# A hybrid decoder block on one Trainium2 core: the first token half normed ahead of the second, two of v's seven products beside it, and another issue order at three later stages

## The chip, the cores and the metric

The kernel runs on one core of one Trainium2 chip. The metric is the device time of one execution in microseconds (us). Engines are named as in the profile: PE (TensorE, the matrix engine), DVE (VectorE), ACT (ScalarE), POOL (GpSimd) and SP (SyncE, which here only issues DMAs, in the order of its queue, and waits on a semaphore before a DMA where it must). SBUF is the memory on the chip, PSUM the accumulators behind PE.

## The reference

One layer of a decoder block over 1024 tokens of width 1024, in float32, with three sub-layers. Every sub-layer norms its input (RMSNorm), and norms its output again before it is added to the stream.

1. Token mixing. One projection h @ w_in is split into q, k, v of a stick-breaking attention (16 heads), into z, x|B|C and dt of a state-space mixer (32 heads, 4 groups, chunks of 128 tokens), and into two gates. Each branch is projected to 1024 columns, gated, summed, and projected once more.
2. Cross-attention with 4 heads of 256 to 256 memory tokens.
3. A SwiGLU feed-forward with 2816 hidden columns.

The part of the reference that bears on this change is this:

```python
h = rms_norm(x, g_pre_mix[l])
q, k, v, z, xbc, dt_raw, ga, gs = _split(h @ w_in[l], IN_SIZES)
...
o_ssm = ssd_branch(z, xbc, dt_raw, ...)
merged = sigmoid(ga) * (o_att @ w_br_att[l]) + sigmoid(gs) * (o_ssm @ w_br_ssm[l])
x = x + rms_norm(merged @ w_mix_out[l], g_post_mix[l])
h = rms_norm(x, g_pre_xa[l])
x = x + rms_norm(memory_cross_attention(h, mem_n, w_xq[l], w_xkv[l], w_xo[l]), g_post_xa[l])
```

## The kernel before

**Products in three passes.** A float32 operand is split into a high part, rounded to PE's fast float32 form (`hi_sb`, on ACT or POOL), and the rest (`lo_of`, on DVE or POOL). A product is then three matmuls: high by high, high by low, low by high.

**Seven products for eight.** The projections of the first sub-layer go by the Winograd form of Strassen's scheme: the normed tokens are cut into four blocks of 512 features by 512 tokens, b11, b21 (the first token half) and b12, b22 (the second), and the weights into four blocks as well. Seven products of sums of them replace eight. The sums on the token side are t1 to t4. They need both halves: t1 = b12 - b11, t2 = b22 - t1, t3 = b22 - b12, t4 = b21 - t2. Their high and low parts stay in SBUF; those of b12 go to scratch in DRAM (`hb_d`).

**The first stage** (L262 to L351). Chunks of 128 tokens are normed: ACT squares and sums (L301), POOL makes the reciprocal root in two small operations (L166, L167), DVE scales (L302), PE turns eight blocks of 128 x 128 (L308). `chunk_pair` does this for chunk c of the first half and chunk c + 4 of the second at once, makes all parts of both (L319 and L320 in `put`, L325, L331 to L336), and multiplies both with the dt columns (`pdt`, L99 to L101, 48 small matmuls for the pair, stored to `dt_d` at L349). Four pairs run; no product of v runs beside them.

**v and z** (L353 to L457). `token_major` makes one third of v|z at a time, 512 + 512 columns. Its weights come in four blocks of two loads of 512 KB each (`zr`, L268). The order of the products is b11, t2, b21, t1, t3, b22, t4. Each product is four steps in k; a step splits one 128 x 512 piece of weights and feeds 12 matmuls, so a product is 48 matmuls. t2's weights are s2 = a21 + a22 - a11, and s1 = a21 + a22 and s3 = a11 - a21 are made first (L416 to L420, DVE for the first third). For the first third all eight loads are issued ahead of the norms, from a pool of ten tiles.

**The feature-major part** (from L461) makes x|B|C, gates, q and k in pairs of 128 columns. `winograd_weights` (L188) loads two tiles `wr` (L194) and makes four sums of weights on POOL (L197 to L200), then splits seven weights. For the first pair POOL splits the first three of them. Its tiles lie where the pools of v and z lay.

**The state-space stage** (from L846). `prep(n)` for one chunk and group loads rows of a small matrix (`colrows`, `keyrows`), whose product (`dec`, L922) holds the exponents of the decay. Both tiles hold constant rows beside the loaded ones: eight rows of a unit matrix come by DMA (`own`, L865) and the loaded sums stand in rows 0 and 1 (L914). `memory` (L1040, L1045) loads and norms the 256 memory tokens; it stands ahead of the loop that calls `prep`.

**The merge** (from L1186) multiplies the attention's output with w_br_att; weights come through `load_split` (L106, tiles `wraw`, `whi`). **Cross-attention** (from L1302) makes all queries, then loads v's projection of the memory (`vx_d`), then the scores (`soft`, L1338 to L1344), their turns (L1352) and the mix.

**What sets the order.** Each engine runs its own instructions in a fixed order that a scheduler worked out when the kernel was built, from the order in which the code issues them, their dependences and the tiles of the pools. A tile that is used again waits for its last reader; a pool that is opened where another one was closed waits for the readers of that space.

Of the kernel before, what the change touches and what calls it, by code (L numbers as in the profile page):

```python
# [30 lines left out]
FILL_LEFT, FILL_RIGHT = 128, 224  # L31
# [3 lines left out]
def hybrid_block(ctx, tc, a, out, dbg=None):  # L35
# [84 lines left out]
    pst0 = ExitStack()  # L120
    prp = pool(pst0, "prm")
    prm1 = mk(prp, [P, P], F32, "prm1")
    prm2 = mk(prp, [P, P], F32, "prm2")
    V.memset(prm1, 0.0)
    V.memset(prm2, 0.0)
    nc.sync.dma_start(prm1[0:96, :], a["conv_w"][0].rearrange("t (f p) -> (t f) p", p=P))
    rows = {}
    r0 = 0
    for nm, n in (("conv_b", 24), ("g_ssm_norm", 16)):
        nc.sync.dma_start(prm2[r0:r0 + n, :], a[nm][0].rearrange("(f p) -> f p", p=P))  # L130
        rows[nm] = r0
        r0 += n
    prmT = mk(cp, [P, 256], F32, "prmT")
    with tc.tile_pool(name="ps_prm", bufs=2, space=PSUM) as pp:
        for i, t in enumerate((prm1, prm2)):
            ps = mk(pp, [P, P], F32, "pprm")
            T.transpose(ps, t, ident)
            V.tensor_copy(prmT[:, i * P:(i + 1) * P], ps)
    pst0.close()
# [9 lines left out]
    nc.sync.dma_start(dsk, a["d_skip"][0].partition_broadcast(P))  # L149

# [3 lines left out]
    G.memset(mone, -1.0)  # L154
    stats = pool(ctx, "stats", 16)
# [96 lines left out]
    with ExitStack() as pa:  # L252
# [8 lines left out]
        rp = pool(pz, "zraw", 10, side="right")  # L261

        def block(r0, c0):
# [8 lines left out]
        def blocks(c0):  # L272
            return block(0, c0), block(0, c0 + HALF), block(512, c0 + HALF), block(512, c0)

        with ExitStack() as p1:
            t4 = pool(p1, "t4x0", 4)
            tt = pool(p1, "tcomb", 6)
            bt = pool(p1, "b12t", 4)
            mp = pool(p1, "memp")
            mt4 = pool(p1, "t4mem", 2)  # L280
            psp = pool(p1, "ps1", 2, PSUM)
            gx = load_gain(mp, "g_pre_mix")
# [6 lines left out]
            for c in (0, 4, 1, 5):  # L289
                load_x(c)  # L290
            wd = mk(mp, [P, KT, 32], F32, "wd")
            nc.sync.dma_start(wd, colblock(w_in, C_DT, 32))
            wdh, wdl = [mk(mp, [P, KT, 32], F32R, n) for n in ("wdh", "wdl")]
# [3 lines left out]
            def normed(c, eng):  # L297
# [13 lines left out]
            def chunk_pair(c):  # L311
# [31 lines left out]
                for i, q in enumerate(((q11, q21), (q12, q22))):  # L343
                    for k in range(KT):
                        hi, lo = q[k // 4]
                        mm3(pdt[0:32, i * P:(i + 1) * P], wdh[:, k, :], wdl[:, k, :], hi[:, k % 4, :], lo[:, k % 4, :], k == 0, k == KT - 1)
# [1344 lines left out]
```

## Time and profile before

| | |
|---|---|
| runs | 2629.86, 2631.71, 2632.2 us (median 2631.71) |
| the profiled execution | 2629.05 us, span 2627.3 us, mean granted PE clock 0.985 |
| PE busy | 2512.0 us, 96% of the span |
| DVE, ACT, POOL busy | 1821.2, 1152.6, 883.5 us |
| data moved by DMA | 271.86 MB, mean 103 GB/s |
| first transposes of tokens on PE | at 13.34 us |
| first product of v on PE | at 56.57 us |
| first matmul of the feature-major part | at 287.67 us |
| `dec` after its longest wait | at 1126.93 us |

How to read it: times are from the start of the span. A row of the waits names the engine and the instruction that waited, who released it, and the us in total, times and longest. A row of a timeline gives start and duration, and in brackets the idle time ahead of it with its releaser. Rows of groups give busy time, mean ns of one, and the idle time ahead. Rows of windows give for a stretch its length and then, engine by engine, busy time and (x) instructions, then the granted PE clock as a share of full speed, the share of the DMA engines and the GB/s.

### The profile page before, as it was taken

To read this page: it belongs to the slowest core of one execution; us is meant where nothing else is said; L and a number is where in the kernel's file an instruction comes from. 1 tells how busy PE (TensorE), PEld (TensorE's weight loads), DVE (VectorE), ACT (ScalarE), POOL (GpSimd) and SP (SyncE) were. 2 spreads that over 40 slices of the span, in tenths; PEclk is the share of its full clock that TensorE was granted. 3 is DMA by queue.
4 is the path that set the end of the run, shared out by engine and by line. 5 is a ranking of instruction groups with operands and counts; after the bars stand their busy time and mean duration, and the time that the engine had idled before them with its cause. 6 is when DMAs were issued, how large, how long until landed. Compare 5 with 4: busy or idle time off the path is not lost. (4 is left out here: it accounts for less than half of the span.)

```text
span 2627.3 us, 32746 instructions
## 1 busy us (share of the span) xinstructions
PE 2512.0 (96%) x12090; PEld 2082.1 (79%) x12090; DVE 1821.2 (69%) x2125; ACT 1152.6 (44%) x2044; POOL 883.5 (34%) x678
## 2 busy tenths in 40 slices
PE   5999999999999999989999999998999999999997
PEld 4888887787788888777888878887787888887786
DVE  7456778766598898677888654415459666666997
ACT  5333455555466665455544312314333333333342
POOL 5212544443111211154555230101114333324763
PEclk8999999999999999989999999999999999999999
DMA  5331442433422322255322461321232232324223
GB/s 174 113 108 53 129 139 91 120 104 105 121 71 70 84 69 69 85 172 183 110 90 70 129 198 66 118 75 41 88 117 72 77 96 73 96 73 152 96 107 134
DMA packets 240491, 271.86 MB, mean 103 GB/s; under 512 B 14751, under 2 KB 171048, under 8 KB 239946
## 3 DMA queue, kind: packets, MB, share of 16 engines
q1 hardware_dynamic: 240330, 269.76, 32.2%
q8 instruction: 95, 1.56, 0.2%
q14 instruction: 66, 0.54, 0.1%
HBM read 192.37 MB, written 68.82 MB: 99 GB/s over the span
## 5 line engine op out<-in xcount | busy, mean ns | idle before, releaser
L733 DVE TENSOR_TENSOR_SCAN n<-n,mask 128x128 f32<-128x128 f32 (+7 forms) x128 | 176.7, 1405 | 10.1 <-ACT n L732 7.1
L96 DVE TENSOR_TENSOR sw<-sf,sw 128x512 fp32r<-128x512 f32 x150 | 132.4, 895 | 64.5 <-ACT sw L93 64.2
L197 POOL TENSOR_TENSOR sf<-wr,wr 128x512 f32<-128x512 f32 x38 | 59.6, 1570 | 271.3 <-DMA wr<-in_w_gu_dram 125.8
L93 ACT ACTIVATE sw<-sf 128x512 fp32r<-128x512 f32 x150 | 92.1, 626 | 115.4 <-PE mm L223 96.9
L752 ACT ACTIVATE wth<-tr,mone 128x512 fp32r<-128x512 f32 x192 | 111.0, 581 | 72.2 <-PE tr L749 70.6
L753 DVE SCALAR_TENSOR_TENSOR wtl<-tr,wth 128x512 fp32r<-128x512 f32 x192 | 101.6, 546 | 38.8 <-ACT wth L752 37.4
L93 ACT ACTIVATE sw<-wr 128x512 fp32r<-128x512 f32 x113 | 71.0, 629 | 128.9 <-PE mm L223 126.8
L223 PE MATMUL mm<-h,sw 128*128 128x512 f32 x320 | 124.3, 389 | 1.2 <-DVE sw L96 1.2
L221 PE MATMUL mm<-h,sw 128*128 128x512 f32 x320 | 122.2, 390 | 2.9 <-ACT h L93 1.5
L222 PE MATMUL mm<-h,sw 128*128 128x512 f32 x320 | 124.6, 389 | 0.3 <-DVE h L96 0.3
L99 PE MATMUL mm<-oth,bw 128*128 128x512 f32 (+1 forms) x320 | 121.2, 379 | 0.1
L101 PE MATMUL mm<-oth,bw 128*128 128x512 f32 (+1 forms) x320 | 118.7, 372 | 1.4 <-DVE bw L96 1.3
L96 DVE TENSOR_TENSOR sw<-wr,sw 128x512 fp32r<-128x512 f32 x113 | 101.6, 900 | 25.9 <-ACT sw L93 17.9
L100 PE MATMUL mm<-otl,bw 128*128 128x512 f32 (+1 forms) x320 | 118.1, 369 | 0.0
L96 DVE TENSOR_TENSOR zl<-zr,zh 128x512 fp32r<-128x512 f32 x84 | 67.6, 810 | 72.0 <-ACT zh L93 71.9
L501 DVE SCALAR_TENSOR_TENSOR b<-b,prmT,b 128x1023 f32<-128x1023 f32 (+2 forms) x72 | 107.2, 1489 | 13.4 <-ACT b L499 12.7
L166 POOL TENSOR_SCALAR rstd<-ms 128x1 f32<-128x1 f32 x82 | 34.6, 422 | 236.0 <-ACT x L1239 110.0
L89 POOL TENSOR_SCALAR v<-va 128x512 fp32r<-128x512 f32 x16 | 20.1, 1260 | 275.1 <-PE av L762 148.0
L732 ACT ACTIVATE n<-sc 128x512 f32<-128x512 f32 (+1 forms) x192 | 89.3, 486 | 48.3 <-PE sc L731 24.4
L93 ACT ACTIVATE zh<-zr 128x512 fp32r<-128x512 f32 x84 | 52.4, 630 | 113.5 <-PE mb L407 55.3
L99 PE MATMUL p<-bw,h 128*128 128x512 f32 x256 | 98.9, 391 | 3.3 <-DVE x L1241 2.4
L101 PE MATMUL p<-bw,h 128*128 128x512 f32 x256 | 100.1, 392 | 0.0
(593 smaller groups left out, 8274.9 us busy)
## 6 DMA issues: line engine op xcount, KB each, us to landing
wr<-in_w_gu_dram SPq DMA_DIRECT2D x80, 256.0 KB
wr<-in_w_in_dram SPq DMA_DIRECT2D x36, 512.0 KB
zr<-in_w_in_dram SPq DMA_DIRECT2D x24, 512.0 KB
gu_d<-t SPq DMA_DIRECT2D x44, 256.0 KB
wraw<-in_w_in_dram SPq DMA_DIRECT2D x20, 512.0 KB
x<-in_x_dram SPq DMA_DIRECT2D x16, 512.0 KB
zs_d<-zo SPq DMA_DIRECT2D x32, 256.0 KB
xs_d<-b SPq DMA_DIRECT2D x32, 256.0 KB
```

What stands on the lines that cost most here:

```text
L93: A.activation(o, i, AF.Copy)
L96: eng.tensor_tensor(o, i, hi.bitcast(F32), ALU.subtract)
L99: first = T.matmul(ps, sh, mh, start=start, stop=False)
L100: T.matmul(ps, sh, ml, start=False, stop=False)
L101: T.matmul(ps, sl, mh, start=False, stop=stop)
L221: T.matmul(ps, w[0][:, k, :], b[0][:, k, :], start=first and k == 0, stop=False, skip_group_check=True)
L222: T.matmul(ps, w[0][:, k, :], b[1][:, k, :], start=False, stop=False, skip_group_check=True)
L223: T.matmul(ps, w[1][:, k, :], b[0][:, k, :], start=False, stop=last and k == 3, skip_group_check=True)
L501: V.scalar_tensor_tensor(acc[:, sh:], y[:, :S - sh], cw(3 - sh, f), acc[:, sh:], ALU.mult, ALU.add)
L733: V.tensor_tensor_scan(nt[:, 0:L][:, ::-1], nt[:, 0:L][:, ::-1], mask[:, S - L:][:, ::-1], 1.0, ALU.mult, ALU.max)
L752: A.activation(wh[:, t0 * P:], pt[:, t0 * P:], AF.Identity, bias=mone)
L753: V.scalar_tensor_tensor(wl[:, t0 * P:], pt[:, t0 * P:], -1.0, wh[:, t0 * P:].bitcast(F32), ALU.add, ALU.subtract)
```

## The change

**First stage.** The columns of the small parameters (`columns`) are made beside the first half instead of ahead of everything. The first token chunk is the first DMA, and ACT runs one Square on a 128 x 1 tile (`warm`) before any token has come. `chunk_pair` is replaced by `first_half` (chunks 0 to 3) and `second_half` (chunks 4 to 7). The turned x11 and x21 of the first half are kept whole in SBUF (`xsv`), and t1 and t4 take them from there. dt is done chunk by chunk (`dt_raw`). The products b11 and b21 of v's first third are made as a list of eight steps, and two of them are issued in each second half; their weights have tiles and PSUM banks of their own. The tiles for b12's parts are single, the PSUM tiles of the turns three instead of six, the scratch of the Square takes a tile of the six of the sums (`tc`).

```diff
-            raw0 = blocks(C_V)
             for c in range(4):
-                chunk_pair(c)
-                if c + 2 < 4:
-                    load_x(c + 2)
-                    load_x(c + 6)
+                dts_.append(first_half(c))
+                if c == 0:
+                    a11 = block(rv, 0, C_V)
+                load_x(c + 4)
+                if c == 1:
+                    columns(psp, "tr")
+                    a12 = block(rv, 512, C_V)
+                if c > 0:
+                    dts_.pop(0)()
+            pa0 = [mk(psa, [P, HALF], F32, "ma") for _ in range(4)]
+            steps = product(pa0, a11, "b11", True, False) + product(pa0, a12, "b21", False, True)
+            for c in range(4):
+                dts_.append(second_half(c))
+                for _ in range(2):
+                    steps.pop(0)()
+                dts_.pop(0)()
+                if c == 1:
+                    u0 = copied(pa0)
+            dts_.pop(0)()
```

**The rest of v and z.** The blocks a21 and a22 come from a pool of their own (`zraw2`), which is opened after the first stage's pools are closed.

```diff
         with ExitStack() as p1:
-            kp = pool(p1, "zk", 9)
+            rp = pool(p1, "zraw2", 6)
+            kp = pool(p1, "zk", 6)
...
+                if j == 0:
+                    b11_, b12_ = a11, a12
+                    b21_, b22_ = block(rp, 0, c0 + HALF), block(rp, 512, c0 + HALF)
+                else:
+                    b11_, b21_, b22_, b12_ = block(rv, 0, c0), block(rp, 0, c0 + HALF), block(rp, 512, c0 + HALF), block(rv, 512, c0)
```

On SP, at the start of the program, the rows of before are these (x: token chunks; wd: the columns of dt; zr: v's weights in 512 KB loads).

```order
L287 DMA x_30_178<-in_x_dram 128x1024 [waits DMAHW0_49]
L292 DMA wd_180<-in_w_in_dram 128x8x32 [waits DMAHW1_49]
L268 DMA zr_186<-in_w_in_dram 128x2x512 [waits DMAHW2_49]
L268 DMA zr_188<-in_w_in_dram 128x2x512 [waits DMAHW3_49]
L268 DMA zr_190<-in_w_in_dram 128x2x512 [waits DMAHW4_49]
L268 DMA zr_192<-in_w_in_dram 128x2x512 [waits DMAHW5_49]
L268 DMA zr_194<-in_w_in_dram 128x2x512 [waits DMAHW6_49]
L268 DMA zr_196<-in_w_in_dram 128x2x512 [waits DMAHW7_49]
L268 DMA zr_198<-in_w_in_dram 128x2x512 [waits DMAHW0_49]
L268 DMA zr_200<-in_w_in_dram 128x2x512 [waits DMAHW1_49]
```

Now the four loads that t2's weights need stand at the end of the first stage on SP (zr_864 to zr_870 are a21 and a22; b12h and b12l are parts of the last chunk, du is dt of the last chunk).

```order
L379 DMA hb_d_75<-b12h_730 512x1x128 [waits DMAHW7_49,Activation_49]
L379 DMA hb_d_76<-b12l_731 512x1x128 [waits DMAHW0_49,Pool_49]
L268 DMA zr_864<-in_w_in_dram 128x2x512 [waits DMAHW1_49,DVE_49,PE_49]
L268 DMA zr_866<-in_w_in_dram 128x2x512 [waits DMAHW2_49,DVE_49]
L356 DMA dt_d<-du_810 32x128 [waits DMAHW3_49,Activation_49]
L268 DMA zr_868<-in_w_in_dram 128x2x512 [waits DMAHW4_49]
L268 DMA zr_870<-in_w_in_dram 128x2x512 [waits DMAHW5_49,PE_49]
L426 DMA v_d<-zk_860 1x512 [waits DMAHW6_49,Pool_49]
```

They moved from ahead of the norms to behind the last chunk's stores. On ACT, the last chunks of the first stage now stand so (x_68 is chunk 7, tc_624 is t2 of chunk 6).

```order
L344 ACTIVATE b22h_116<-tr_618 128x4x128 [waits DVE_49]
L344 ACTIVATE t3h_125<-tc_625 128x4x128
L344 ACTIVATE t2h_123<-tc_624 128x4x128 [waits DVE_49]
L332 ACTIVATE tc_708,ms_709<-x_68_360 128x1024 [waits DMAHW3_49]
L344 ACTIVATE t4h_127<-tc_626 128x4x128 [waits DVE_49]
L355 ACTIVATE du_782<-pdt_783 32x128 [waits DMAHW0_49,PE_49]
L374 ACTIVATE tc_727<-tr_715 128x512 [waits PE_49,Pool_49]
```

The Square of chunk 7 (L332) stands behind the high part of t2 of chunk 6, and the same row stands so for chunk 6 behind chunk 5. On PE all 96 matmuls of the two products stand ahead of the turns of chunk 6.

**Between z and the feature-major part** the `wr` loads moved on SP. Before, around the last stores of z (`zs_d`):

```order
L377 DMA zs_d<-zo_2306 128x512 [waits DMAHW6_49,DVE_49]
L377 DMA zs_d<-zo_2306 128x512 [waits DMAHW7_49,DVE_49]
L194 DMA wr_2456<-in_w_in_dram 128x4x256 [waits DMAHW0_49,Activation_49,Pool_49]
L194 DMA wr_2457<-in_w_in_dram 128x4x256 [waits DMAHW1_49,Pool_49]
L194 DMA wr_2601<-in_w_in_dram 128x4x256 [waits DMAHW2_49]
L377 DMA zs_d<-zo_2380 128x512 [waits DMAHW3_49,DVE_49]
L377 DMA zs_d<-zo_2380 128x512 [waits DMAHW4_49,DVE_49]
```

and now:

```order
L434 DMA zs_d<-zo_2342 128x512 [waits DMAHW7_49,DVE_49]
L434 DMA zs_d<-zo_2416 128x512 [waits DMAHW0_49,DVE_49]
L434 DMA zs_d<-zo_2416 128x512 [waits DMAHW1_49,DVE_49]
L434 DMA zs_d<-zo_2427 128x512 [waits DMAHW2_49,DVE_49]
L434 DMA zs_d<-zo_2427 128x512 [waits DMAHW3_49,DVE_49]
L191 DMA wr_2496<-in_w_in_dram 128x4x256 [waits DMAHW4_49,PE_49,Pool_49]
L191 DMA wr_2497<-in_w_in_dram 128x4x256 [waits DMAHW5_49,Activation_49,Pool_49]
```

The tile zo_2416 of the kernel now is zo_2380 of the kernel before: the loads moved behind four more stores, which wait for sums of the last but one product.

**The state-space stage.** The constant rows are written by POOL and DVE in place, at partitions 0, 32 and 64, so the four `own` DMAs go. `prep(0)` and `prep(1)` are called ahead of `memory`.

```diff
+        HEADS, ONES = (0, 32), 64
...
+            G.memset(t.bitcast(F32), 0.0)
         for t in colrows:
-            V.tensor_scalar(t, tri, 0.0, None, ALU.mult)
-            for j in range(2):
-                nc.sync.dma_start(t[2 + j * GH:2 + (j + 1) * GH].bitcast(F32), own[0:GH])
...
+        for n in range(AHEAD):
+            prep(n)
         for m in range(2):
             memory(m)
```

On SP, before (sum_d: the sums for the first two chunks; g_mem and mem: the memory's tokens):

```order
L1040 DMA bw_10074<-in_g_mem_dram 128x1024 [waits DMAHW4_49,PE_49]
L1045 DMA wraw_10076<-in_mem_dram 128x1024 [waits DMAHW5_49,DMAHW0_49]
L1045 DMA wraw_10098<-in_mem_dram 128x1024 [waits DMAHW6_49]
L914 DMA colrows_2040_10058<-sum_d 1x8x128 [waits DMAHW7_49]
L914 DMA colrows_2040_10058<-sum_d 1x8x128
```

and now:

```order
L927 DMA keyrows_2052_10098<-key_d 8x512 [waits DMAHW0_49]
L963 DMA colrows_2050_10096<-sum_d 1x8x128 [waits DMAHW1_49]
L963 DMA colrows_2051_10097<-sum_d 1x8x128 [waits PE_49]
L1089 DMA bw_10112<-in_g_mem_dram 128x1024 [waits DMAHW3_49,PE_49]
L963 DMA colrows_2051_10097<-sum_d 1x8x128 [waits DMAHW4_49]
L1094 DMA wraw_10177<-in_mem_dram 128x1024 [waits DMAHW5_49]
L1094 DMA wraw_10199<-in_mem_dram 128x1024 [waits DMAHW6_49]
```

The loads of the first sums moved ahead of the three loads of the memory.

**Merge and cross-attention.** The weights of w_br_att are taken by `branch_weights`, one block ahead, the first one issued ahead of the loads of o_d. Two of the sixteen query products move in between the scores of the first four chunks, and the loads and splits of vx_d move behind these scores, with the high parts on ACT.

```diff
+        ws = {0: branch_weights(0)}
...
         for f in range(KT):
-            whi, wlo = load_split(wp, colblock(a["w_br_att"][0], f * P), [P, KT, P], 2)
+            if f + 1 < KT:
+                ws[f + 1] = branch_weights(f + 1)
+            whi, wlo = ws.pop(f)
...
         for c in range(4):
             soft(c)
+            if c % 2:
+                query(KT - 2 + c // 2, 1)
```

Beside these, one filler tile that shifts the addresses in SBUF is 96 instead of 128 bytes long.

More of the change, by code (lines that the diff above doesn't have):

```diff
@@ L154, in hybrid_block @@
     G.memset(mone, -1.0)
+    warm = mk(cp, [P, 1], F32, "warm")
+    A.activation(warm, mone, AF.Square)
     stats = pool(ctx, "stats", 16)
@@ L384, in token_major, with bank @@
             def token_major(j, c0, put, i0):
-                a11, a21, a22, a12 = raw0 if j == 0 else blocks(c0)
-                banks = ["ma", "mb"][::1 if j % 2 == 0 else -1]
+                bb = ((psa, "ma"), (psb, "mb"))[::1 if j % 2 == 0 else -1]
+                def bank(x):
+                    pl, tag = bb[x]
+                    return [mk(pl, [P, HALF], F32, tag) for _ in range(4)]
                 def both(fn):
@@ L409, in bank, with times @@
-                def bank(x):
-                    return [mk(psp, [P, HALF], F32, banks[x]) for _ in range(4)]
-                pa_ = bank(0)
-                product(pa_, a11, "b11", True, False)
+                def times(*args):
+                    for f in product(*args):
+                        f()
+                if j == 0:
[3 more added lines that the diff above has]
+                    b11_, b21_, b22_, b12_ = block(rv, 0, c0), block(rp, 0, c0 + HALF), block(rp, 512, c0 + HALF), block(rv, 512, c0)
@@ L414, in token_major @@
+                if j == 0:
+                    pa_, u = pa0, u0
+                else:
+                    pa_ = bank(0)
+                    times(pa_, b11_, "b11", True, False)
                 s1 = [mk(rp, [P, 2, HALF], F32, "zr") for _ in range(2)]
                 E_ = V if j == 0 else G
-                both(lambda q: E_.tensor_tensor(s1[q], a21[q], a22[q], ALU.add))
-                s3 = a21
-                both(lambda q: E_.tensor_tensor(s3[q], a11[q], a21[q], ALU.subtract))
-                s2 = a11
@@ L420, in token_major @@
[L420 to L429 removed]
+                both(lambda q: E_.tensor_tensor(s1[q], b21_[q], b22_[q], ALU.add))
@@ L432, in token_major @@
                 pb_ = bank(1)
[L433 removed]
+                times(pb_, s1, "t1", True, False)
                 for c in range(4):
@@ L436, in token_major @@
                 pa_ = bank(0)
-                product(pa_, s3, "t3", True, False)
+                times(pa_, s3, "t3", True, False)
                 w = []
@@ L441, in token_major @@
                     V.tensor_tensor(w[c], u[c], pb_[c], ALU.add)
-                product(pb_, s4, "b22", False, True)
+                times(pb_, s4, "b22", False, True)
                 for c in range(4):
@@ L445, in token_major @@
                     put(c + 4, i0 + 1, w[c])
-                product(pa_, a22, "t4", False, True)
+                times(pa_, b22_, "t4", False, True)
                 for c in range(4):
```

259 lines of the change are left out of this document (142 added, 117 removed).

## The prediction

> **What bounds the kernel now.** I read the page's busy times first.
>
> ```profile
> PE 2512.0 (96%) x12090; PEld 2082.1 (79%) x12090; DVE 1821.2 (69%) x2125; ACT 1152.6 (44%) x2044; POOL 883.5 (34%) x678
> ```
>
> PE is busy for 2512.0 of the span's 2627.3 us, and the change leaves the products as they are. So the change can only move the 115.3 us in which PE waits, and what a lower clock costs behind a wait. The waits of PE, second, name the ones that the change touches.
>
> ```profile
> PE tr L308 <- DVE x L302: 13.9, 5, 8.7
> ...
> PE dec L922 <- DMA colrows<-sum_d: 5.1, 1, 5.1
> ...
> PE tr L1352 <- DVE prob L1344: 4.2, 2, 3.4
> PE mm L99 <- ACT whi L93: 4.1, 1, 4.1
> ...
> PE p L1338 <- ACT prob L1342: 2.5, 2, 1.7
> ```
>
> The first row is the first stage, the second the state-space stage, the fourth the merge, the third and fifth cross-attention. Third, windows, for the first stage and for the clock behind a wait (PE busy is the second number, PEclk the sixth entry).
>
> ```profile
> 0.00:56.60 56.60, 27.59 (x259) 24.15 (x259) 41.12 (x49) 32.10 (x60) 35.58 (x42) 0.84 0.60 201
> 56.60:76.60 20.00, 20.00 (x77) 16.30 (x78) 11.17 (x14) 8.61 (x15) 3.56 (x3) 0.87 0.04 8
> 67.30:78.00 10.70, 10.70 (x48) 8.84 (x48) 4.24 (x5) 4.32 (x8) 3.24 (x2) 1.00 0.17 51
> 288.00:308.00 20.00, 18.90 (x82) 14.95 (x81) 15.73 (x19) 10.04 (x18) 12.34 (x9) 1.00 0.48 141
> 1115.00:1150.00 35.00, 25.11 (x114) 18.69 (x113) 29.36 (x35) 21.76 (x38) 18.23 (x14) 0.78 0.54 174
> 1126.90:1130.40 3.50, 3.47 (x9) 2.75 (x10) 2.91 (x2) 3.47 (x7) 3.34 (x4) 0.52 0.53 174
> ```
>
> PE idles 29.0 us of the first 56.6. One product, 48 matmuls, takes 10.70 us at full clock, 0.223 each. Right behind the 5.1 us wait in the state-space stage the granted clock is 0.52 for 3.5 us: such a wait costs 1.7 us more than itself. The Trainium skill, "TensorE: Matmul & The Clock Gate", Part 1, says that the clock halves after an idle window of some 3.4 us and recovers after a busy one; this row agrees (0.52 for 3.50 us).
>
> **The first stage.** Head. The chain to the first turn before:
>
> ```profile
> 2.94 1.98 SPq L287 DMA_DIRECT2D x<-in_x_dram  x4
> 5.64 8.41 SPq L268 DMA_DIRECT2D zr<-in_w_in_dram  x8
> 8.55 1.28 ACT L301 ACT_TABLE_LOAD   x1 [8.55 <-DMA x<-in_x_dram]
> 9.85 1.06 ACT L301 ACTIVATE junk<-x 128x1024 bf16<-128x1024 f32 x1
> 13.34 4.03 PE L308 MATMUL tr<-ident,x 128*128 128x128 f32 x16 [8.68 <-DVE x L302]
> ```
>
> x0 is the sixth DMA at 2.94 and the Square starts at 9.85, behind a table load of 1.28 that began when x had come. Now x0 is the first DMA, 2.2 us earlier, alone at first, and `warm` takes the table load before: Square at about 4.5 (bounds 4 and 6.3, the old distance of 5.6 from issue), first turn 13.34 - 9.85 = 3.5 later, at 8.0. That is a gain of 5.3.
>
> Up to chunk 5 and both products PE has 96 product matmuls, 21.4 us, and three quarters of the turns and dt matmuls that made its 27.59 us before: 20.7 at the clock of that window, 10.4 if that had been half clock throughout. From 8.0 that ends between 39.8 and 50.1. I take 48, near the upper end, since some short waits will be left.
>
> Then comes what the change costs. Chunks 6 and 7 have no product left beside them (the order has all 96 matmuls ahead of chunk 6's turns), and the Square of a chunk stands on ACT behind the high part of t2 of the chunk before. So their chains run one after the other. The groups of the window 0 to 57 price the chain.
>
> ```profile
> L302 DVE SCALAR_TENSOR_TENSOR x<-x,rstd,g_pre_mix 128x1024 f32<-128x1024 f32 x8 | 12.9, 1610 | 9.3 <-POOL rstd L167 9.3
> L301 ACT ACTIVATE junk<-x 128x1024 bf16<-128x1024 f32 x8 | 8.3, 1044 | 0.0
> L166 POOL TENSOR_SCALAR rstd<-ms 128x1 f32<-128x1 f32 x8 | 7.5, 942 | 10.4 <-ACT junk L301 9.9
> L96 POOL TENSOR_TENSOR b<-tc,b 128x512 fp32r<-128x512 f32 x4 | 5.6, 1389 | 0.0
> L167 POOL TENSOR_TENSOR rstd<-rstd,mhalf 128x1 f32<-128x1 f32 x8 | 5.5, 682 | 0.6
> ...
> L334 DVE TENSOR_TENSOR tc<-tr,tc 128x512 f32<-128x512 f32 x4 | 2.7, 680 | 0.0
> ...
> L319 ACT ACTIVATE t2h<-tc 128x512 fp32r<-128x512 f32 x4 | 2.5, 628 | 1.8 <-DVE tc L334 1.7
> ```
>
> Square 1.04 and its read-out 0.2, the root 0.94 + 0.68, scaling 1.61, eight turns 1.3 (a third of 4.03 for sixteen, which ran in part at half clock), copy and high part of b12 on ACT 2 x 0.63, its low part on POOL 1.39, t3 on DVE 0.68, high part of b22 on ACT 0.63, its low part and t2 on DVE 2 x 0.68, high part of t2 0.63: 11.7. These means hold waits of POOL and DVE on each other that fewer operations at a time may lessen, and no hand-offs, so I take 11.8 for a chunk. From below the bound is 7: the POOL and DVE work of a half if chunks overlapped (four low parts of 1.39 and the root). Two chunks from 48: t2's high part of chunk 7 at 71.6, its dt on PE and `du` on ACT at about 73.
>
> Last, the loads of a21 and a22. Before, their rows (5.64 above, eight in 8.41 us) stood ahead of the norms and the sums were made beside them. Now they stand on SP behind chunk 7's b12 parts and its last dt store, so zr_868 is issued at about 73.5. In the state-space rows below 1.5 MB and the sums behind it took 6.4 us from the issue, so for the 1 MB of two loads I take 4: 77.5. This is the DVE row for the sums:
>
> ```profile
> L416 DVE TENSOR_TENSOR zr<-zr,zr x2: 1272/1476/1681, 25.5 to 29.0; 128x1024 f32<-128x1024 f32 x2
> ```
>
> Four of them stand before the first half of s2, 4 x 1.27 = 5.1, then a split of 0.6: t2 starts at 83.2, PE having waited 10 us, and its first 3.5 us run at half clock (+1.7): as if at 84.9. Before, b11 started at 56.6; the window 56.60 to 76.60 holds 77 matmuls where 90 fit, 2.9 lost, so b11 and b21 would be done at 56.6 + 2.9 + 21.4 = 80.9. **First stage: +4** (if chunks take 7: -6; if sums take 1.7 and chunks 12.5: +8).
>
> **From z to the feature-major part.** Before:
>
> ```profile
> 270.62 1.58 SPq L194 DMA_DIRECT2D wr<-in_w_in_dram  x3
> 277.63 14.94 SPq L377 DMA_DIRECT2D zs_d<-zo  x7
> 277.12 1.64 POOL L197 TENSOR_TENSOR sf<-wr,wr 128x512 f32<-128x512 f32 x1 [45.19 <-DVE zk L449]
> 282.11 1.74 POOL L200 TENSOR_TENSOR sf<-wr,sf 128x512 f32<-128x512 f32 x1
> 285.21 0.63 POOL L89 TENSOR_SCALAR sw<-wr 128x512 fp32r<-128x512 f32 x1 [1.36 <-PE ma L407]
> 286.98 1.29 POOL L96 TENSOR_TENSOR sw<-wr,sw 128x512 fp32r<-128x512 f32 x1
> 287.67 0.39 PE L221 MATMUL mm<-b11h,sw 128*128 128x512 f32 x1
> ```
>
> The first pair's weights come off POOL, four sums from 277.12 to 283.85, then high parts and low parts, just in time for PE at 287.67. Now the loads stand behind the four stores that begin at 277.63 and wait for DVE until about 282.8; the issue is at 283.5, and the tiles land 4 us later, at 287.5. Four sums take 5.2 to 6.9 (1.29 is the row of a POOL operation by itself, 1.64 to 1.74 those of the sums), three high parts some 1.8, the first low part 1.3; a few matmuls go between. Weights flow at about 296, so PE waits about 7.5 from 287.7, in place of the 1.1 that it idles in the window from 288 to 308: +6.4, and 1.7 for the clock behind it. **+8** (+5 to +12; nothing else is in PE's queue there but first-pair matmuls).
>
> The rows of 1.64 to 1.74 against 1.29 are what the Trainium skill, "SBUF — State Buffer", section "Who interferes with whom", describes: a DVE instruction with both inputs in SBUF and a POOL instruction that reads SBUF exclude each other. By this rule the sums of z (silu times x on DVE, both in SBUF) would hold POOL back by one such op each, and the term would lie at its upper end, +10 to +12.
>
> **State space.**
>
> ```profile
> 1119.65 0.84 SPq L1045 DMA_DIRECT2D wraw<-in_mem_dram  x2
> 1120.55 1.30 SPq L914 DMA_DIRECT2D colrows<-sum_d  x2
> 1126.93 1.22 PE L922 MATMUL dec<-colrows,keyrows 128*128 128x512 f32 x2 [5.07 <-DMA colrows<-sum_d]
> ```
>
> The first sums were issued behind 1.5 MB of memory tokens, and PE waited 5.07 for them. Now they are ahead, and the four own-row DMAs are gone; that wait and its 1.7 of clock can go. But DVE is busy 29.36 of the 35 us here, so what is late next is DVE's share: at most 5.6 can be won, and POOL's memsets and the later memory loads cost some. **-4** (-6.8 to +1).
>
> **Cross-attention.** Two query products, 24 matmuls each at 0.22, now lie where PE waited for the scores' exponents, 2.5 in all. The 3.4 for DVE's prob stays: it is not moved. **-2** (-3 to 0). **Merge.** The 4.1 stays: on SP w_br_att's load stands behind the same gate loads as before. **0** (-5.8 if it goes, with its clock).
>
> **Sum:** 4 + 8 - 4 - 2 = +6 on the profiled execution's 2629.05, so 2635.05. It lies 2.66 under the median of the runs, 2631.71; on the median I say **2637.7**. A measurement can tell about 0.2% from no change, 5.3 us here.
>
> **Rivals.** *The first stage pays off* (faster): chunks 6 and 7 overlap at 7 us each and the four sums are done while PE still has dt to do. Place: PE between the last product matmul and t2; it decides when that idle time stays under 16 us (the forecast has 26: 2 x 11.8 of chunks less 7 of their own PE work, and 10 before t2; a gain from this stage beyond -6 needs 10 less). First stage -6, feature-major start at its low +5, state space -6.8, cross-attention -3: -11, 2621. For it: POOL's work of a half is 7 at most. Against: the ACT order above.
>
> *Gains and losses cancel* (same): the first stage 0, the rest +8 - 4 - 2: +2, 2634. For it: the 48 is the softest number of the sum, and 4 us less there do it.
>
> *Locks add up* (slower than forecast): DVE and POOL exclude each other in the chunks (942 ns on average for a step on one column, 128 x 1) and in the feature-major start: +8 + 12 - 4 - 2 = +14, 2646.
>
> *The change does not do what it says*: the state-space wait remains, since the sums' tiles now wait for POOL's memsets. Then +10, 2642.
>
> **Chances.** Forecast (+3 to +9) 0.42, cancel 0.25, pays off 0.17, locks 0.10, wait remains 0.06. Faster by over 0.2% (under 2626.4): 0.18; slower by over 0.2% (over 2637.0): the upper two thirds of the forecast and both slow rivals, 0.50; the rest 0.32. The range reaches from the middle of the faster rival, 2621, to 2648.
>
> **What would show it.** Right: first turn near 8, products gapless to about 48, two waits of some 4 us and one near 10 before t2 at 83, a wait of about 7.5 at the first `mm` behind z with POOL's L194 as its source, no `dec` wait above 2 us. Wrong: t2 starting under 75, or the feature-major matmuls following z without a gap; then the sum is negative.

## The result, and the profile after

The changed kernel took 2649.4 us (median of six runs, 2646.06 to 2655.75), the kernel before beside it 2629.9 (2624.66 to 2632.2): a ratio of 1.008, with a 95% interval from 1.0065 to 1.0094. It is slower by some 20 us, where I had said 6 with a range up to 2648. The direction was right, the size was not.

The profiled execution of the changed kernel took 2655.75 us, with a span of 2654.0; it is the longest of its six, 6.4 us over their median, and one part below shows a likely reason. Its page:

```profile
PE 2519.6 (95%) x12090; PEld 2085.9 (79%) x12090; DVE 1827.7 (69%) x2118; ACT 1158.9 (44%) x2061; POOL 874.8 (33%) x684
```

PE's work grew by 7.6 us for the same 12090 matmuls, at a mean granted clock of 0.981 instead of 0.985, and its idle time by 19.1, to 134.4. The waits of PE name the places.

```profile
PE tr L339 <- DVE x L333: 16.4, 3, 8.0
PE mb L287 <- ACT zh L93: 14.0, 1, 14.0
...
PE mm L218 <- POOL sw L89: 6.6, 1, 6.6
PE mm L99 <- DVE qs L727: 6.1, 5, 1.5
...
PE tr L1413 <- DVE prob L1405: 4.1, 2, 3.4
PE mm L99 <- ACT both L93: 4.0, 1, 4.0
...
PE p L1399 <- ACT prob L1403: 0.6, 1, 0.6
```

The first row is the head (8.0) and the chains of chunks 6 and 7 (4.1 and 4.3). The 14.0 is t2, the 6.6 the first feature-major pair, both forecast, the first of them too small. The waits for `qs` were not forecast. The 5.1 of `dec` and most of the 2.5 of the scores' exponents are gone, the 4.1 of the merge and the 3.4 of `prob` stayed, as said.

To see where the time went I take the same instruction in both traces. The first columns are the times in the trace of before and of after.

| first instruction of | before | after | difference |
|---|---|---|---|
| t2's product (before: third product of v) | 80.95 | 86.45 | +5.5 |
| the fourth product | 91.83 | 102.58 | +10.7 |
| the feature-major part | 287.67 | 305.14 | +17.5 |
| attention's scores | 689.72 | 711.69 | +22.0 |
| the state-space stage (`dec`) | 1114.57 | 1142.91 | +28.3 |
| the merge | 1513.60 | 1542.20 | +28.6 |
| cross-attention's scores | 1710.38 | 1738.03 | +27.6 |
| the feed-forward | 1998.59 | 2024.73 | +26.1 |
| end of the span | 2627.27 | 2653.97 | +26.7 |

These are two single traces. The 10.7 and the 17.5 come again within 1 us in `first_only`, `after_split_va` and `ssm_late` below, which leave the first stage as it is. The 4.5 that are lost between the feature-major start and the scores do not: `first_only`, with the same code there, takes 402.1 us for it, as long as the kernel before, where this trace takes 406.6. What cost it here is open.

The timeline of the changed kernel around t2, SP's loads, DVE's sums and low parts, and POOL's s4 (rows of the four engines):

```profile
69.55 2.32 SPq L268 DMA_DIRECT2D zr<-in_w_in_dram  x2
73.91 0.93 SPq L268 DMA_DIRECT2D zr<-in_w_in_dram  x2
80.98 1.23 DVE L468 TENSOR_TENSOR zr<-zr,zr 128x1024 f32<-128x1024 f32 x1 [7.70 <-DMA zr<-in_w_in_dram]
85.66 1.22 DVE L470 TENSOR_TENSOR zr<-zr,zr 128x1024 f32<-128x1024 f32 x1
85.82 3.27 POOL L480 TENSOR_TENSOR zr<-zr,zr 128x1024 f32<-128x1024 f32 x1 [10.68 <-DVE zr L472]
86.45 2.08 PE L287 MATMUL mb<-zh,t2h 128*128 128x512 f32 x4 [14.03 <-ACT zh L93]
86.79 2.85 DVE L96 TENSOR_TENSOR zl<-zr,zh 128x512 fp32r<-128x512 f32 x1
89.70 0.79 PE L288 MATMUL mb<-zl,t2h 128*128 128x512 f32 x1 [1.17 <-DVE zl L96]
```

The second pair of loads left at 73.91, as forecast (73.5), but DVE got the first of the two 7.1 us later, not 4. And t2's first low part, a DVE operation of 0.7 us, took 2.85 beside POOL's s4 (`s4_late` below takes s4 away), and the next one stood behind another sum. Windows over t2's product:

```profile
86.40:89.90 3.50, 2.28 (x5) 1.36 (x6) 3.50 (x3) 0.52 (x2) 2.69 (x1) 0.50 0.00 0
89.90:97.60 7.70, 7.70 (x23) 6.08 (x23) 6.58 (x7) 3.08 (x6) 2.76 (x1) 0.62 0.43 118
93.30:95.60 2.30, 2.30 (x7) 1.82 (x6) 2.30 (x4) 0.63 (x1) 0.32 (x1) 0.50 0.50 191
95.70:97.60 1.90, 1.90 (x10) 1.54 (x9) 0.87 (x2) 0.26 (x1) 0.00 (x0) 1.00 0.81 200
```

Only 5 matmuls ran in the first 3.5 us, and DVE was busy for all of that time. The clock was 0.50 until about 95.7 and full from there on: 9 us of t2's product, where I had reckoned 3.5. The product took 16.1 us, 5.2 more than the 10.9 of the third product in the kernel before. Of these, 1.2 are the wait at 89.70, and the 8.1 us in which PE worked at 0.50 cost some 4 (an estimate from these rows).

The feature-major start, SP, POOL and PE:

```profile
291.21 1.56 SPq L191 DMA_DIRECT2D wr<-in_w_in_dram  x3
297.75 1.29 POOL L194 TENSOR_TENSOR sf<-wr,wr 128x512 f32<-128x512 f32 x1 [55.08 <-DMA wr<-in_w_in_dram]
302.35 1.71 POOL L197 TENSOR_TENSOR sf<-wr,sf 128x512 f32<-128x512 f32 x1
305.14 0.79 PE L218 MATMUL mm<-b11h,sw 128*128 128x512 f32 x1 [6.55 <-POOL sw L89]
```

This is the forecast's mechanism row by row: late loads, four sums on POOL, the high part, then PE. It costs 6.8 us at the first matmul.

### The profile page after: what moved, and what is told of

It reads as the page before. It is cut to its first block, busy times and chain, and to the rows that moved or that the text cites. A ratio compares the mean times of both kernels' runs of the same rounds, so it can differ in the third digit from the quotient of the medians.

```text
span 2654.0 us, 32762 instructions
## 1 busy us (share of the span) xinstructions
PE 2519.6 (95%) x12090; PEld 2085.9 (79%) x12090; DVE 1827.7 (69%) x2118; ACT 1158.9 (44%) x2061; POOL 874.8 (33%) x684
## 5 line engine op out<-in xcount | busy, mean ns | idle before, releaser
L784 DVE TENSOR_TENSOR_SCAN n<-n,mask 128x128 f32<-128x128 f32 (+7 forms) x128 | 184.3, 1463 | 12.2 <-ACT n L783 11.3
```

The source lines that it names most:

```text
L784: V.tensor_tensor_scan(nt[:, 0:L][:, ::-1], nt[:, 0:L][:, ::-1], mask[:, S - L:][:, ::-1], 1.0, ALU.mult, ALU.max)
```

## The experiments

My theory after the result: all of the loss that is the change's own lies ahead of the feature-major part, 10.7 from the first stage and 6.8 from the start of the feature-major part, and the 6 us in attention are a matter of chance. The rivals: the later stages carry some of the loss, or the late loads are not what makes t2 late.

### One half of the change at a time

`first_only` is the kernel before with the change's parts up to the end of z, `rest_only` the kernel before with its state-space, merge and cross-attention parts.

> The kernel before with the first stage, v and z of the change alone (state space, merge and cross-attention as before). Theory: the loss lies in the first 310 us. Between the first product and the first feature-major matmul PE loses what the changed kernel's trace showed, 305.1 against 287.7, so +17 to +18 there, and 0 to +10 in attention by how often POOL's va subtraction takes the shared port ahead of DVE's scan: 2647 to 2655, ratio 1.007 to 1.010. Rival 1 (the later stages lose): only the first stage's forecast +12 is left, 2642, ratio 1.0045. Rival 2 (the loss in attention comes from a changed state-space, merge or cross-attention part, by addresses): attention pairs at 49.6 us here.

> The kernel before with the changed state-space, merge and cross-attention parts alone. Theory: start and attention as before, cross-attention -3, state space 0 (the wait for the first sums goes and comes back as waits on ACT and DVE), merge 0: 2627, ratio 0.999. Rival 1 (state space gains as I forecast): -7, 2623, ratio 0.997. Rival 2 (the later parts carry some of the loss): over 2635, ratio over 1.002.

`first_only` took 2646.73 us, ratio 1.0075 (1.0061 to 1.0088): +19.4 on the 2627.35 of before beside it. Its first feature-major matmul stands at 304.69, +17.0, and the end of its span at +17.7. `rest_only` took 2630.29, ratio 1.0007 (0.9997 to 1.0018): no change that can be measured. So the loss lies in the first 305 us, and rival 1 of `first_only` falls.

The state-space part does nothing although the wait that I wanted gone is gone. The first 40 us of that stage in the changed kernel, and the whole of it:

```profile
1142.90:1182.90 40.00, 32.12 (x166) 25.37 (x167) 39.24 (x44) 28.37 (x50) 28.81 (x25) 0.87 0.56 173
1142.90:1542.20 399.30, 380.82 (x2064) 322.48 (x2064) 305.72 (x372) 201.99 (x374) 196.01 (x185) 0.98 0.41 127
```

and in the kernel before:

```profile
1114.60:1154.60 40.00, 29.81 (x153) 23.39 (x153) 34.00 (x41) 24.08 (x42) 18.97 (x15) 0.80 0.54 173
1114.60:1513.60 399.00, 378.73 (x2067) 321.62 (x2066) 307.58 (x372) 201.35 (x374) 194.90 (x181) 0.98 0.41 128
```

DVE is busy for 39.24 of the 40 us, and PE works just 2.3 us more in them, in place of the 5.1 of the wait; the stage as a whole takes 399.3 instead of 399.0. In `rest_only`, the waits that came in its place are for ACT and DVE:

```profile
PE ptr L994 <- ACT s L981: 2.1, 1, 2.1
PE dec L894 <- ACT s L921: 2.1, 1, 2.1
...
PE po L99 <- DVE s L966: 1.9, 1, 1.9
...
PE dec L920 <- DVE colrows L866: 1.3, 1, 1.3
```

### The chance in attention

In attention PE's `qs` waits come from one DVE operation in each head pair, a scan of 128 x 512, which meets POOL's subtraction of `va`. POOL's subtraction is released by a DMA and the scan by ACT, and they become ready within some 0.2 us of each other. The two engines in the kernel before, in one head pair:

```profile
763.65 1.21 DVE L733 TENSOR_TENSOR_SCAN n<-n,mask 128x512 f32<-128x512 f32 x1
763.85 3.21 POOL L710 TENSOR_TENSOR va<-va,vb 128x1024 f32<-128x1024 f32 x1 [4.92 <-DMA va<-v_d]
```

and in the changed kernel's profiled run:

```profile
785.53 2.38 POOL L761 TENSOR_TENSOR va<-va,vb 128x1024 f32<-128x1024 f32 x1 [4.66 <-DMA va<-v_d]
785.60 3.40 DVE L784 TENSOR_TENSOR_SCAN n<-n,mask 128x512 f32<-128x512 f32 x1
```

Whoever comes first holds the port, and the other one waits. In the trace of before DVE came first in five of six pairs, in the trace of after POOL did. PE waits only where DVE loses. The section "Who interferes with whom" of the Trainium skill's page "SBUF — State Buffer" says that a DVE instruction with two inputs in SBUF and a POOL instruction that reads SBUF exclude each other, and that the order of issue decides who blocks; these rows agree: 1.21 against 3.40 us for the same scan. Two runs cut POOL's operation into four, in the changed kernel and in the kernel before:

```diff
-                    G.tensor_tensor(va, va, vb, ALU.subtract)
+                    for c in range(0, NCH, 2):
+                        G.tensor_tensor(va[:, c:c + 2], va[:, c:c + 2], vb[:, c:c + 2], ALU.subtract)
```

> The changed kernel with POOL's va subtraction of 128x1024 in each head pair cut into four of 128x256. Theory (a toss for the shared port): no DVE scan of 128x512 in attention over 2.0 us (3.4 in five of six pairs before the cut), head pairs at 49.6 us instead of 51.5, waits for qs under 0.5 us; the total falls by 4 to 8 to 2642 to 2645, ratio 1.005 to 1.006. Rival (the loss in attention has another cause): scans of 3.4 or head pairs over 51 stay, ratio 1.008.

> The kernel before with the same cut of POOL's va subtraction. Theory: DVE's scan won the port in five of six pairs of the profiled run, so little is left to win: -2 to 0 us, and runs closer to each other (before: 2624.7 to 2632.2). Rival (four operations of POOL cost more than one and delay v): slower by 2 us or more.

The groups of this scan between 720 and 1110 us, in the changed kernel and with the cut in it:

```profile
L784 DVE TENSOR_TENSOR_SCAN n<-n,mask 128x512 f32<-128x512 f32 x16 | 29.2, 1824 | 0.2 <-ACT n L783 0.2
```

```profile
L785 DVE TENSOR_TENSOR_SCAN n<-n,mask 128x512 f32<-128x512 f32 x15 | 19.3, 1288 | 0.2 <-ACT n L784 0.2
```

The mean falls from 1824 to 1288 ns, and attention from the first scores to `dec` takes 425.7 us instead of 431.2, level with the 424.9 of before. The totals, 2647.03 with a ratio of 1.0069 (1.0056 to 1.0082), and 2625.96 with 0.9999 (0.999 to 1.0007), moved less than 3 us and within their intervals; the expected fall by 4 to 8 was too much. In eight other traces with the new first stage and POOL's operation whole, DVE lost none to two of the six pairs, and attention took 424.5 to 426.7 us; in `s4_late` it lost four, and attention took 429.4. So the length of attention follows the lost pairs, and the change need not cost anything there. Rival 2 of `first_only` foretold what that run shows, attention without the loss; but `wr_act` and `ssm_late`, which have the changed later parts too, are free of it as well (424.6 and 424.5), so this rival falls. Whether the change makes a lost pair likelier is not shown: four or five were lost in two of ten such traces, at most one in the three with the old first stage.

### The late loads and the sums

`t2_loads` puts the blocks a21 and a22 into the token tiles of the chunks 4 to 7 as these come free, so that they are loaded one by one beside the norms. `t2_sums` also makes the first half's sums ahead of the last chunk.

```diff
+            def early_load(c):
+                t = mk(t4, [P, D], F32, "x4").rearrange("p (k f) -> p k f", k=2)
+                r0 = (0, 512)[c % 2] + c // 2 * 256
+                nc.sync.dma_start(t, w_in[r0:r0 + 256, C_V + HALF:C_V + 2 * HALF].rearrange("(k p) f -> p k f", p=P))
+                (b21e, b22e)[c % 2].append(t)
...
+                early_load(c)
+                if c == 2:
+                    s1e = mk(rp, [P, 2, HALF], F32, "zr")
+                    V.tensor_tensor(s1e, b21e[0], b22e[0], ALU.add)
+                    V.tensor_tensor(b21e[0], a11[0], b21e[0], ALU.subtract)
+                    V.tensor_tensor(a11[0], s1e, a11[0], ALU.subtract)
```

> The changed kernel with the four loads of a21 and a22 put into the tiles of the second half's token chunks, so that they are issued one by one as those chunks are turned, ahead of each chunk's stores; the six sums stay in their place behind the last chunk. Theory (the loads behind the last stores are half of the 14.0 us wait, the five sums of DVE ahead of s2 the other half): DVE begins its sums at 72.6 to 73 instead of 81.0, t2 starts at 79 to 80 instead of 86.45, the fourth product at 94 to 96 instead of 102.6: 2641 to 2643, ratio 1.005. Rival (the chain of the last chunks is the whole wait): t2 stays above 84 and the total at 2649.

> The same with the three sums of the first half of the weights made between the third and the fourth second-half chunk (one tile of weight parts less in the first stage, one more later). Theory: t2 starts at 74 to 76, its first product runs in 12 to 14 us instead of 16.1, the fourth product starts at 87 to 89 against 91.8 in the kernel before: the first stage is then 3 to 5 us better than before, and what is left of the loss is the start of the feature-major part and attention: 2634 to 2638, ratio 1.003. Rival (the sums in the chain of the chunks cost there what they save): fourth product over 93.

DVE's sums and PE's t2 in `t2_loads`:

```profile
73.27 3.41 DVE L487 TENSOR_TENSOR zr<-x,x 128x1024 f32<-128x1024 f32 x2
80.81 2.07 PE L288 MATMUL mb<-zh,t2h 128*128 128x512 f32 x4 [8.32 <-ACT zh L93]
```

DVE begins its sums at 73.3 instead of 81.0, and t2 starts at 80.8 instead of 86.45: 5.6 us of the wait were the loads, 8.3 are left to the sums. In `t2_sums` t2 starts at 72.08 with no wait, and the fourth product at 85.91, 5.9 ahead of the kernel before. The totals are 2638.89, ratio 1.0047 (1.0033 to 1.006), and 2633.38, ratio 1.0017 (1.0008 to 1.0026), each a little under what was expected. So with its loads and half of its sums early, the new first stage is 8.9 us ahead of the old one at t2 (72.08 against 80.95), and the late loads and sums turned that into a loss.

### The first feature-major pair

`wr_act` leaves POOL only the four sums of the first pair (the splits go to ACT and DVE), and `wr_free` issues the stores of z's last third from ACT's queue.

```diff
-                pair(*j, 3 if i == 0 else 0)
+                pair(*j, 0)
```

```diff
-                nc.sync.dma_start(zs_d[c * P:(c + 1) * P, i * HALF:(i + 1) * HALF], sg)
+                (nc.scalar if i >= 2 else nc.sync).dma_start(zs_d[c * P:(c + 1) * P, i * HALF:(i + 1) * HALF], sg)
```

> The changed kernel with no weight of the first feature-major pair split on POOL: high parts on ACT, low parts on DVE, sums still on POOL. Theory (the wait is POOL's seven operations behind late loads): the first feature-major matmul comes 0.6 to 1.5 us after the loads have landed, at 298.6 to 300 instead of 305.1, no wait of 6.5; the total falls by 4 to 6 to 2643 to 2645, ratio 1.006. Rival (DVE's and ACT's z work is in the way as much): first matmul after 302, total down by less than 2.

> The changed kernel with the stores of z's last third (zs_d) issued from ACT's queue instead of SP's, so that the wr loads of the first feature-major pair are no longer queued behind stores that wait for DVE. Theory (the place in SP's queue makes the loads late): wr issued before 270, POOL's sums done before PE needs them, no wait over 1.5 us at the first feature-major matmul, which comes at about 299 instead of 305.1; total -5 to -6: 2644, ratio 1.006. Rival (it is POOL or the tiles, not the queue): the wait stays over 4 us. Another risk: ACT is now held up by stores that wait for DVE, and z itself gets slower.

In `wr_act` PE has the first weights at 298.0 and then waits for the first low part:

```profile
298.01 0.50 PE L218 MATMUL mm<-b11h,sw 128*128 128x512 f32 x1 [3.17 <-ACT sw L93]
301.87 0.80 PE L220 MATMUL mm<-b11h,sw 128*128 128x512 f32 x1 [2.29 <-DVE sw L96]
```

Two waits, 5.5 us together, stand for the one of 6.55; the first matmul comes earlier, in part because t2 began 2.8 us earlier in this run, whose loads for t2 came sooner. The total is 2642.86, ratio 1.0055 (1.0042 to 1.0069). `wr_free` on SP and PE:

```profile
283.99 1.48 SPq L191 DMA_DIRECT2D wr<-in_w_in_dram  x3
298.11 0.50 PE L218 MATMUL mm<-b11h,sw 128*128 128x512 f32 x1 [0.32 <-POOL sw L89]
300.92 0.50 PE L218 MATMUL mm<-t1h,sw 128*128 128x512 f32 x1 [2.08 <-POOL sw L89]
```

The long wait is gone, and the total is 2641.66, ratio 1.0049 (1.0034 to 1.0063). But the loads left at 284.0, not ahead of 270: free of the queue they still waited for the space of v's and z's weights (SP's wait ended with a matmul of z, `PE mb L288`). So the queue made them 7.2 us late, from 284.0 to 291.2, and the tiles hold them until 284.0.

That the long wait is gone does not mean that its time is won. This is PE from the end of z over the first 48 feature-major matmuls, in the kernel before, in the changed one and in `wr_free`:

```profile
287.80:300.30 12.50, 11.40 (x49) 8.73 (x48) 9.56 (x13) 5.76 (x12) 7.30 (x6) 1.00 0.54 168
298.60:318.80 20.20, 13.66 (x49) 11.05 (x50) 15.12 (x13) 6.35 (x13) 17.29 (x13) 0.83 0.31 104
297.80:316.10 18.30, 14.83 (x49) 10.90 (x50) 11.70 (x13) 6.33 (x13) 10.64 (x9) 0.81 0.34 115
```

Of the 7.7 us that the change loses there, `wr_free` gives back 1.9 and `wr_act`, with some 19 us, about 1: the weights still come late, and PE waits in smaller pieces at a clock of 0.81. So the falls of both totals, 7 and 8 us by the ratios, are not explained by this place. `ssm_late` below touches neither it nor the first stage and comes out as low.

### All mends together

`mended` is `t2_sums`, `wr_act` and the cut of `va` in one kernel.

> The changed kernel with all three: the early loads and sums, the first pair without POOL's splits, and POOL's va subtraction in four parts. Theory: -15, -5 and 0 to -8: 2622 to 2628, ratio 0.997 to 1.000, level with the kernel before or a little faster, since the first stage is then 3 to 5 us ahead of it and the feature-major start 1 to 2 behind. Rival (a gain at one place comes back as a wait at the next): over 2632.

It took 2635.88, ratio 1.0027 (1.0018 to 1.0036): no better than `t2_sums` alone, so the rival was right here. Its feature-major part begins at 285.48, 2.2 ahead of the kernel before, and attention's scores at 694.57, 4.8 behind it. One of the waits on the way there is this:

```profile
PE sc L808 <- DMA kh<-kh: 4.5, 1, 4.5
```

PE's wait for this small copy of a key tile is 3.6 us longer than in the kernel before (0.83 there). Another 2.3 of the 7 us lie in the first 48 feature-major matmuls, 14.9 us from the first on against 12.6. The rest I did not take apart.

### The slow product of t2

`warm_pe` keeps PE at work ahead of t2, `s4_late` makes the sums s4 of v on DVE.

```diff
+                if j == 0:
+                    for _ in range(44):
+                        T.matmul(pb_[0], hb["t2"][0][:, 3, 384:512], hb["t2"][0][:, 3, :], start=True, stop=True, skip_group_check=True)
```

```diff
-                both(lambda q: G.tensor_tensor(s4[q], b12_[q], s2[q], ALU.subtract))
+                if j > 0:
+                    both(lambda q: G.tensor_tensor(s4[q], b12_[q], s2[q], ALU.subtract))
...
+                if j == 0:
+                    both(lambda q: V.tensor_tensor(s4[q], b12_[q], s2[q], ALU.subtract))
```

> The changed kernel with 44 matmuls on PE between the last dt matmul and t2 that overwrite each other in a bank which t2's product then begins anew: they only keep PE at work, some 11 us of the 14 us wait. Theory (part of t2's slow product, 16.1 us for 48 matmuls, is the clock, which after the 14.0 us wait was 0.50 to 0.62 for 11 us): granted clock 0.9 or more in t2, its product in 12 to 13 us, fourth product at 99 instead of 102.6, total -3 to -4: 2645, ratio 1.0065. Rival (t2's product is held by DVE, whose two last sums and locked low parts stand between its steps): product still 15 us or more, total unchanged.

> The changed kernel with the two sums s4 of v's third made on DVE, in line, instead of on POOL beside t2's low parts. Theory (each POOL sum of 2.8 to 3.3 us holds the port and stretches a low part of 0.7 to 2.85 or more; in line it costs DVE 1.2): t2's product in 14 to 15 us instead of 16.1, fourth product at 100.5 to 101.5 instead of 102.6 where t2 starts at 86.4. Rival (the clock alone makes t2 slow): product unchanged at 16.

`warm_pe`, windows over t2's product:

```profile
86.30:89.80 3.50, 1.46 (x5) 0.94 (x6) 3.50 (x3) 0.44 (x1) 2.61 (x1) 0.78 0.00 0
89.80:93.20 3.40, 3.40 (x9) 2.63 (x9) 3.30 (x3) 2.19 (x4) 2.53 (x1) 0.50 0.22 34
```

The clock was 0.78 in the first window, PE did the same 5 matmuls and waited for DVE, and the clock fell to 0.50 afterwards; the product took 15.9 us, about as in the changed kernel, and the total did not fall: 2654.64, ratio 1.0094 (1.0081 to 1.0107). My theory of the clock alone failed. `s4_late`, its first window, a later one, and DVE's first low part:

```profile
86.30:89.80 3.50, 2.71 (x6) 1.71 (x7) 3.50 (x4) 1.12 (x2) 0.00 (x0) 0.50 0.00 0
91.50:93.20 1.70, 1.70 (x10) 1.37 (x9) 1.70 (x4) 1.49 (x3) 0.00 (x0) 1.00 0.62 153
```

```profile
88.43 0.68 DVE L96 TENSOR_TENSOR zl<-zr,zh 128x512 fp32r<-128x512 f32 x1
```

With POOL's two sums away (its column is 0.00) the low part takes 0.68 instead of 2.85, the clock is full by 91.5 instead of 95.7, and the product takes 13.25 us instead of 16.1. So POOL's s4 made 2.9 of the 5.2 us, and most of it through the clock: PE, fed more slowly, worked at 0.50 for 8.1 us instead of about 4. The 2.3 that are left come behind the wait of 14.3 us that this run has too; they were not taken apart. The total is 2644.38, ratio 1.0051 (1.0036 to 1.0066), a fall of more than these 2.9.

### The order of the state-space stage, and two more versions

`ssm_late` calls prep(0) and prep(1) behind `memory` again in the changed kernel. `before_head` is the kernel before with the head alone: x0 the first DMA, `warm`, and `columns` beside the second chunk pair. `best2` has the changed first stage with early loads and sums, s4 on DVE, z's last stores on ACT, and the old later stages.

> The changed kernel with the first two calls of prep behind memory again, as before (the constant rows are still made without DMAs). Theory (DVE and ACT bound that stretch, so the wait for the first sums costs nothing): the wait of about 5 us at dec returns, and the state-space stage up to the merge stays at 399 us within 2 (before 399.0, changed 399.3). Rival (my forecast, a gain of 4 to 7 that something else ate): the stage gets 4 to 7 us longer, to 403 or more, total 2654.

> The kernel before with the head of the change alone: first token chunk as the first DMA, the table load taken early, parameter columns made beside the first stage; chunk pairs and all else as before. Theory (the old first stage is a chain of chunk pairs that starts with the first turn): first turn at 8 instead of 13.3, first product of v at 52 to 53.5 instead of 56.6, and that is kept to the feature-major part, where the loads have slack: -3 to -5, 2623 to 2625, ratio 0.998 to 0.999, faster than both kernels. Rival (the second half of each pair now comes later, since four chunks and the gain share the DMA): first product at 56 or later, no gain.

> The changed first stage with early loads and sums (as in t2_sums), s4 on DVE, z's last stores on ACT's queue (as in wr_free), and the old state-space, merge and cross-attention parts. Theory: fourth product at 85 to 86 (-6 against the kernel before), first feature-major matmul at 282 to 284 (-4 to -5), and the end within 2 us of that lead or less as the feature-major part gives some back: 2623 to 2628, ratio 0.998 to 1.000. Rival (the feature-major part is bound by DVE and POOL and gives all back): 2630 or more.

In `ssm_late` the wait did not come back as a whole (`dec` waits 1.6), so it does not settle what that wait was worth; the stage took 394.3 us, 5 less than in the changed kernel, and the total is 2642.33, ratio 1.005 (1.0038 to 1.0062). The rival, 403 or more, falls: no gain of the calls ahead shows. But stages with the calls ahead took 395.2 to 402.1 in the other traces, so 5 us less isn't shown to be the order's doing. The total fell by 8 us against the changed kernel's ratio, as far as in `wr_free`, `wr_act` and `s4_late`, and no run says why; a fall of this size in a total is not by itself a proof of the cause that a run was made for. `t2_loads` lies level with these; `t2_sums`, `mended` and `best2` lie clearly below.

`before_head` begins its turns at 7.83 and its feature-major part 2.5 us earlier than before, and took 2626.96, ratio 0.999 (0.9982 to 0.9999): just clear of no change, and 2.2 us under the 2629.15 of before beside it where 3 to 5 were expected. More than half of the 5.5 won at the head is lost again ahead of the first product of v, which comes at 54.16 instead of 52 to 53.5: in the chain of pairs PE waits 1 us more and works 2 us longer, 29.0 us against 26.8.

`best2` took 2636.84, ratio 1.0022 (1.0013 to 1.0032): no gain. Its fourth product stands at 86.00, 5.8 ahead, but its first pair waits again:

```profile
279.87 16.12 SPq L191 DMA_DIRECT2D wr<-in_w_in_dram  x5
```

```profile
291.94 0.79 PE L218 MATMUL mm<-b11h,sw 128*128 128x512 f32 x1 [9.21 <-POOL sw L89]
```

The stores are off SP's queue here too, and the loads leave 2.9 us before PE ends z; in `wr_free` they left 13.8 us before that. What differs is where the tiles of v and z lie; that these hold the loads back is argued from it and not tested. The lead is lost at this wait, and not later in the feature-major part as the rival had it: PE comes to the scores at 694.19, 4.5 behind the kernel before, as it began that part 4.3 behind.

## Why the prediction was wrong

Point by point, by its own steps.

- **Head, chunks, chains**: right. First turn at 8.02 (8.0 forecast), PE at work until 49.3 (48), chunks 6 and 7 in 11.6 us each (11.8), with waits of 4.1 and 4.3 ahead of their turns.
- **"First stage: +4"**: this step failed. It measured +10.7 at the fourth product. It was mis-sized in two terms. The loads: "for the 1 MB of two loads I take 4" was 7.1 for the first of the two. I took two thirds of 6.4 us for 1.5 MB, and left out that the first pair of loads, issued from 69.55 on, and two stores to `v_d` are under way beside them. The stores alone are not the cause: in `wr_act` they go out at the same times, and DVE has the load after 4.3 us (73.94 to 78.20), against 6.2 to 7.4 in the other seven traces with these loads in their place. Ahead of it the issue of the first pair took 1.1 us in `wr_act` and 2.3 here; whether that makes the difference is open. And "its first 3.5 us run at half clock (+1.7)": the product took 16.1 us, 5.2 more than the 10.9 of before, half clock for 9 us, since two sums were left to DVE and POOL's s4 held up its low parts. `s4_late` gave 2.9 of these back. I had weighed the lock in the chunks and in z, where it did little, and not here. The two terms, 3.1 and 3.5, make up nearly all of the 6.7 that were missing. (The two products done at 80.95 in the kernel before are b11 and t2, not b11 and b21; the sum needs only that they are two.)
- **"From z to the feature-major part", +8**: right in size, 6.8 at the first matmul and 7.7 after 48, and right in mechanism, but two of its steps were off and cancel. The loads left 7.4 us ahead of z's end, not 4.2, and POOL began its sums 6.5 us after that, not 4. The upper end, +10 to +12 by the lock, did not come: the four sums took 6.3 us, within the 5.2 to 6.9. The late issue had a second cause beside the queue, the tiles, as `wr_free` showed.
- **"State space: -4"**: failed. 399.3 against 399.0 us, and 1.0007 (0.9997 to 1.0018) in `rest_only`. The wait went, and waits for ACT and DVE took all of its place and not just a part; DVE had been named as late next.
- **"Cross-attention: -2"**: not settled. The stage took 1.5 us less in the trace, but 2.5 less in `first_only`, which has the old one. **Merge 0**: right, 4.04 waited.
- **Attention** was no term. In the profiled run it cost 6.4, by the five lost pairs; the medians hold little of it.

By the terms: 10.7 + 6.8 at the feature-major part, then 0, make 17.5. On the median to which the forecast was added, 2631.71, that gives 2649.2, beside the measured 2649.4. That this fits so closely is luck: the kernel before measured beside it took 2629.9, so the change cost 19.5, and 2 us of it are in no term.

Of the chances, "slower by over 0.2%" adds up to 0.44 from its parts (0.28 + 0.10 + 0.06), not to 0.50. Of the rivals, "locks add up" had the right engines and named 2646, with 0.10, but placed the lock in the chunks and not at t2. "Pays off" failed by its own sign: PE was idle for 26.5 us between the last product matmul and t2 (26 forecast, under 16 needed), 12.5 of it in the chains and 14.0 at t2, and the chunks did not overlap. That the stage gains 8.9 us at t2 when its loads and sums come early is another mechanism.

## What to carry to other kernels

A stage that is made shorter by moving work into it may also have moved out what was hidden there: here four prefetched loads and six sums, worth more than the stage won. When a forecast prices a stall, price what runs just behind it too: the operations that pile up there meet on DVE and POOL at once, and PE, fed in drips, is slow for longer than the stall's own length tells. When a run takes a wait away, see in its trace when the work behind the wait is done, not just that the wait is gone: here it came back in small pieces. And a difference in one profiled run at a place that the change doesn't touch is first to be looked for in a second run.

## What the runs showed of the hardware

- DVE's scan and POOL's subtraction in attention become ready within 0.07 to 0.2 us of each other, and by who comes first the same scan takes 1.21 or 3.40 us. In the traces with the new first stage attention took 424.5 to 426.7 us with none to two of six scans lost, 429.4 with four and 431.2 with five, by the same code.
- Behind a wait of 14.0 us the granted clock stayed at 0.50 for 9 us where PE had 5 matmuls in the first 3.5 us, and for less than 5 where they came faster (`s4_late`: a wait of 14.3 us, t2 from 86.95, full by 91.5). In `warm_pe`, where PE had been kept at work, its mean was 0.78 in these 3.5 us with 5 matmuls, and 0.50 in the next window.
- With the same loads and stores issued around it, a load of 512 KB reached DVE 4.3 us after its issue in one trace (`wr_act`) and 6.2 to 7.4 us in seven others. So t2's start, by the same code of the first stage, lay between 83.67 (`wr_act`) and 86.95 (`s4_late`).
